# A plain weight tile between the two passes of an output projection, and raw weights of every third pair in two other tiles

## The chip, the cores and the metric

The kernel runs on one core of one Trainium2 chip. The metric is the device time of one execution in microseconds (us); the reported time is the median of several executions. A core has a matrix engine (PE, with its weight loads shown apart as PEld), a vector engine (DVE), a scalar engine (ACT), a general engine (POOL) and a queue engine (SP) that issues most DMAs here. Each engine works through its own instruction list in order and waits on semaphores.

## The reference

One encoder layer over 512 tokens of width 1024, in float32:

```python
h = swiglu(rmsnorm(x, g1), w1_in, w1_out);  x = x + 0.5 * rmsnorm(h, g1p)      # D_FF = 2816
h = mixer(rmsnorm(x, gm), ...);             x = x + rmsnorm(h, gmp)            # convolution and mLSTM heads
h = swiglu(rmsnorm(x, g2), w2_in, w2_out);  x = x + 0.5 * rmsnorm(h, g2p)
def swiglu(x, w_in, w_out):
    gate, up = split(x @ w_in, 2);  return (silu(gate) * up) @ w_out
```

The two feed-forward blocks (function `ffn`, called twice) hold the work that the change touches; the mixer lies between them and is not touched.

## The kernel before

**Products.** Each float32 operand is split into a rounded high part and a low remainder (`split`: a CAST on ACT for the high part, a subtraction on DVE, L327, for the low part), and a product is three matmuls: high by high, high by low, low by high. `split_free` (L331, L332) is the same with no fixed order. On top of this both projections of a block use a seven-product scheme (as in Strassen's method) for most of the weights, with the combinations of operands formed by DVE subtractions.

**Input projection.** The 2816 hidden columns are 22 tiles of 128 (`NF`); the first two (`PLAIN`) are multiplied plainly (L491), the other 20 (j = 2 to 21) with seven products of 12 matmuls of 256 columns each (`mm_part`, L468). For each j a pair of raw weight tiles (gate g and up u, 512 KB each) is loaded by SP (L178) into two tiles of the pool `rawp`, which has four; `w_pair` (L190, with `split`) makes the operands out of them on DVE and ACT, and the raw tiles are free again when its last split has read them. So the load of a pair waits for the pair two before it.

**Output projection.** The 22 hidden tiles are the contraction. `OUT` lists the order: eight items "a" (a0 to a7, the first pass), then "b" items (the second pass) and plain items "k". An a takes two rows of weights and does products 1, 6, 7, 5; a b takes the second of these rows again and does products 2, 3, 4 (`product_out`, L613; six matmuls of 512 columns to a product). A k multiplies one hidden tile plainly into all eight PSUM banks (`mm_out`, L637, 24 matmuls). With `SEVEN` = 8 and `TAIL` = 5 the order is a0 ... a7, b0, k16, b1 ... b7, k17 ... k21, and k17 to k21 are multiplied at the end, one block of 128 tokens after the other.

**Between the passes.** The eight PSUM banks hold sums of the first pass that must be read out and partly subtracted before the second pass overwrites or goes on with them. `taken(n)` does it after each product of a7: for product 1 a copy on ACT (L623), for 6, 7 and 5 two subtractions each on DVE (L572, `big<-ps,big`), six in all. Product 4 restarts the banks of product 7 and k16 those of product 6; products 2 and 3 go on in the banks of 1 and 5. `left_b` forms the left factors of a group of two b's: one split of 1024 elements (L332 on DVE), one subtraction (L572), one split of 512; `w_out_b` splits the weights of one b (1024 and 512 elements, L327).

**Who orders the instructions.** The program is written in one order; a planner with a timeline model of its own then orders each engine's list, taking an instruction early when its model says it is ready. `pin` ties an instruction behind the one that the program traced just before it on the same engine. `tc.issue_after(x)` ties what a block traces on x's engine behind x. Both set the order in the engine's list only. A new tile of a pool waits until an old one of the pool is free.

**The two idle tiles.** The pool `t4p` has two tiles (`t4()`). In a block they hold normalised inputs, then `v1` and `v3` in `combine_x` (L398), then nothing but `own2` (raw rows for a0 and a1, L159) and the scratch `s1` of `left_a`.

Of the kernel before, what the change touches and what calls it, by code (L numbers as in the profile page):

```python
# [8 lines left out]
F32 = mybir.dt.float32  # L9
# [7 lines left out]
P = 128  # L17
# [8 lines left out]
DV = 128  # L26
EPS = 1e-6
NEG = -1e30
TAIL = 5
SEVEN = 8  # L30
WARM = 20
WARM2 = 4
ON_POOL = (0, 1, 2, 3)
PLAIN = 2
BW = 528


@with_exitstack
def encoder_kernel(ctx: ExitStack, tc: tile.TileContext, a: dict, out: bass.AP):
# [15 lines left out]
    def nm(s):  # L55
        uid[0] += 1
        return f"{s}_{uid[0]}"
# [47 lines left out]
        return [v[0]], v[1]  # L105


    OUT = [("a", i) for i in range(SEVEN)]
    for i in range(SEVEN):
        OUT += [("b", i)] + [("k", 2 * SEVEN + i)] * (2 * SEVEN + i < NF - TAIL)  # L110
    OUT += [("k", k) for k in range(2 * SEVEN, NF) if ("k", k) not in OUT]

    stream = []
    for w_in, w_out in ((w1i, w1o), (w2i, w2o)):
        if w_in is w2i:
            stream += [(wm[blk(i, 2 * P), V0:V0 + 512].rearrange("(k p) f -> p k f", p=P), 2) for i in range(4)]
            stream += [cols(wm, c) for c in (Q0, Q0 + P, K0, K0 + P)]
            stream += [cols(wm, O0 + i * P) for i in range(4)]
            stream += [cols(wm, CG)]
            for i in range(4):  # L120
                stream += [cols(wm, c + i * P) for c in ((CG, HC, BG) if i else (HC, BG))]
            stream += [rows(wo, k * P) for k in MIXK[:5]]
        for j in range(NF):
            pair = [cols(w_in, j * P), cols(w_in, DFF + j * P)]
            stream += pair if j < PLAIN else [([v[0] for v in pair], KD)]
        for kind, n in OUT:
# [8 lines left out]
    pos, done = [0], [0]  # L135

    def w_load(n):
        for _ in range(n):
            if pos[0] < len(stream):
# [27 lines left out]
                if kk == "b":  # L167
                    nc.gpsimd.dma_start(kept[0], aps[0][:, 0:512], accum_op=ALU.add)
                    aps = [aps[0]]
                    own = [kept.pop(0)]  # L170
                else:
                    own = []
                for ap in aps:
                    raw = rawp.tile([P, 1024], F32, tag="raw", name=nm("raw"))
                    if isinstance(kk, str):
                        nc.sync.dma_start(raw[:, 1024 - ap.shape[1]:], ap)
                    else:
                        nc.sync.dma_start(raw if kk == 1 else raw.rearrange("p (k f) -> p k f", k=kk), ap)  # L178
                    raws.append(raw)
# [292 lines left out]
    def ffn(xq, between, finish, mid=None, within=None, ahead=(2, 2, 1, 1), late=None, prep=None):  # L472

# [97 lines left out]
        def tt(o, a_, b_, op, order=lambda v: None):  # L571
            order(nc.vector.tensor_tensor(out=o, in0=a_, in1=b_, op=op))  # L572
# [9 lines left out]
            return [{n: (hi[:, i, c:c + 256], lo[:, i, c:c + 256]) for n, c in at.items()} for i in range(g)]  # L582

        def group(i):
            g = min(2, SEVEN - i)
# [15 lines left out]
        def left_b(i):  # L601
# [4 lines left out]
            split_free(hi[:, :, 512:768], lo[:, :, 512:768], a_[:, :, early])  # L606
            return parts(hi, lo, g, {4: 0, 2: 256, 3: 512})

        def product_out(n, left, right, first, last_):
            tb, half = bank[n]  # L610
            for t in range(2):
                for x, y in ((0, 0), (0, 1), (1, 0)):
                    nc.tensor.matmul(  # L613
                        acc[tb + t][half], left[n][x][:, blk(t)], right[n][y], start=first and x == y == 0,
                        stop=last_ and x == 1, skip_group_check=True)

        def taken(n):

            for t in range(2):
                o = acc[bank[n][0] + t][bank[n][1]]  # L620
                e12, e22, e21 = extra[2 + t, 1], extra[t, 1], extra[t, 0]
                if n == 1:
                    nc.scalar.copy(e12, o)  # L623
                elif n == 5:
                    tt(e22, o, e21, ALU.subtract, pin)
                elif n == 6:
                    tt(e12, o, e12, ALU.subtract, pin)
                else:
                    tt(e21, o, e12, ALU.subtract, pin)

        begun = set()

        def mm_out(tb, half, k, hT, w):
            fresh = (tb, half) in ((0, 1), (1, 1)) and (tb, half) not in begun
            begun.add((tb, half))
            for hh, ww in ((0, 0), (0, 1), (1, 0)):
                nc.tensor.matmul(  # L637
                    acc[tb][half], hT[hh][:, blk(tb)], w[ww][:, blk(half, 512)],
                    start=fresh and hh == ww == 0, stop=k == NF - 1 and hh == 1, skip_group_check=True)
# [12 lines left out]
            acc[at[0]][at[1]] = ps()  # L652
        hs, plain_n = None, 0
        ks = {}
        for at, (kind, n) in enumerate(OUT):
            if kind == "k":
                if plain_n % 2 == 0:
                    hs = bigt(F32R)
                q = 2 * (plain_n % 2)
                plain_n += 1  # L660
                hT = (hs[:, q, 0:512], hs[:, q + 1, 0:512])
                split(hT[0], hT[1], hcol(n))
                ks[n] = (hT, w_get(min(2, len(OUT) - 1 - at)))
                if plain_n == 1 and mid:
                    mid()
                if n < NF - TAIL:
                    for tb in range(NT):
                        for half in range(2):
                            mm_out(tb, half, n, *ks[n])
            elif kind == "a":  # L670
                if n % 2 == 0 and n:
                    lefts = left_a(n)
                left, right = lefts[n % 2], w_get(1)
                for m in ((1, 6, 7, 5) if n else (6, 7, 5)):
                    product_out(m, left, right, n == 0, n == SEVEN - 1)
                    if n == SEVEN - 1:
                        taken(m)
            else:
                if n % 2 == 0:
                    lefts = left_b(n)  # L680
                left, right = lefts[n % 2], w_get(2)
                for m in (2, 3, 4):
                    product_out(m, left, right, n == 0 and m == 4, False)

        ring.clear()
        pinned["rest"] = False
# [11 lines left out]
        if prep:  # L698
            prep()
        for tb in range(NT):  # L700
            todo = [(half, k) for half in ((1, 0) if tb == NT - 1 else (0, 1)) for k in range(NF - TAIL, NF)]
# [505 lines left out]
    def store(tb, h):  # L1207
        nc.sync.dma_start(out[0, blk(tb), h], x_t[tb][:, h])

    ffn(xT3, {(3, 2): lambda: flip_q(3, xs[3], xT3)}, lambda tb, acc: post_norm(tb, acc, g_post3, 4.0, store, (1, 0) if tb == NT - 1 else (0, 1)))  # L1210


_INS = [
# [26 lines left out]
```

## Time and profile before

| what | value |
|---|---|
| runs of the kernel | 899.17, 899.81, 902.55 us; median 899.81 |
| the profiled execution, by its own time | 899.46 us |
| its span, first to last instruction | 897.1 us |
| first input projection, L468 | about 38 to 236 us |
| first output projection | about 234 to 351 us |
| second input projection, L468 | about 571 to 780 us |
| second output projection | about 780 to 891 us |

A row of the timeline is: start in us, time covered in us, engine, line and operation, tile written <- tiles read, shape, count; in square brackets the idle time of the engine before it and who ended it. Successive matmuls overlap: a matmul of 512 columns is shown with some 0.39 us, though the next one starts some 0.23 us after it. A wait for several semaphores is put down to the one that came last.

### The profile page before, as it was taken

To read this page: it belongs to the slowest core of one execution; us is meant where nothing else is said; L and a number is where in the kernel's file an instruction comes from. 1 tells how busy PE (TensorE), PEld (TensorE's weight loads), DVE (VectorE), ACT (ScalarE), POOL (GpSimd) and SP (SyncE) were. 2 spreads that over 40 slices of the span, in tenths; PEclk is the share of its full clock that TensorE was granted. 3 is DMA by queue.
4 is the path that set the end of the run, shared out by engine and by line. 5 is a ranking of instruction groups with operands and counts; after the bars stand their busy time and mean duration, and the time that the engine had idled before them with its cause. 6 is when DMAs were issued, how large, how long until landed. Compare 5 with 4: busy or idle time off the path is not lost.

```text
span 897.1 us, 14998 instructions
## 1 busy us (share of the span) xinstructions
PE 886.2 (99%) x5935; PEld 806.9 (90%) x5935; DVE 696.8 (78%) x1081; ACT 469.9 (52%) x803; POOL 77.7 (9%) x100
## 2 busy tenths in 40 slices
PE   9999999999999999999999999999999999999997
PEld 7999999999987888988888888999999999987885
DVE  5988988888898777574666736889788888898755
ACT  6645555555547644464555435654554555657521
POOL 5000000001140111100011000000000000222000
PEclk9999999999999999999999999999999999999999
DMA  8434443434798570433222601324334334899402
GB/s 237 115 95 119 120 116 105 130 98 123 194 214 224 164 211 1 123 90 94 71 72 71 191 20 50 112 71 123 95 104 126 101 94 136 195 230 228 151 25 93
DMA packets 136079, 110.61 MB, mean 123 GB/s; under 512 B 5045, under 2 KB 115657, under 8 KB 136010
## 3 DMA queue, kind: packets, MB, share of 16 engines
q1 hardware_dynamic: 129354, 97.09, 36.5%
q0 software_dynamic: 6656, 12.58, 8.2%
q8 instruction: 46, 0.75, 0.3%
q14 instruction: 23, 0.19, 0.1%
HBM read 107.56 MB, written 2.10 MB: 122 GB/s over the span
## 4 chain that ended last, share of the span: by engine, by line
PE 82%; DVE 8%; DMA 6%; ACT 2%; issue 2%; POOL 0%; DVEq 0%; POOLq 0%; SPq 0%; ACTq 0%
PE ps L468 40%; PE ps L459 12%; PE ps L613 7%; PE ps L637 7%; PE ps L1197 5%; PE ps L491 4%; DVE wlo L327 3%; PE ps L819 3%; DMA raw<-in_w_ffn_out_dram 2%; DMA t<-in_w_ffn_out_dram 2%; DMA raw<-in_w_ffn_in_dram 2%; DVE big L332 1%; DVE big L572 1%; ACT whi L324 1%; PE ps L1112 1%
## 5 line engine op out<-in xcount | busy, mean ns | idle before, releaser
L468 PE MATMUL ps<-big,whi 128*128 128x256 f32 x1920 | 265.0, 280 | 0.7 <-ACT whi L324 0.7
L324 ACT CAST whi<-raw 128x1024 fp32r<-128x1024 f32 x197 | 202.4, 1051 | 114.3 <-DVE raw L190 46.7
L327 DVE TENSOR_TENSOR wlo<-raw,whi 128x1024 fp32r<-128x1024 f32 x193 | 233.6, 1219 | 35.5 <-ACT whi L324 20.2
L468 PEld LDWEIGHTS ps<-big,whi 128*128 128x128 f32 x1920 | 243.0, 188 | 1.3 <-ACT whi L324 1.1
L468 PE MATMUL ps<-big,wlo 128*128 128x256 f32 x960 | 151.6, 280 | 0.0
L468 PEld LDWEIGHTS ps<-big,wlo 128*128 128x128 f32 x960 | 129.7, 188 | 0.0
L613 PE MATMUL ps<-whi,big 128*128 128x512 f32 x384 | 122.2, 390 | 0.5 <-DVE big L572 0.3
L613 PEld LDWEIGHTS ps<-whi,big 128*128 128x128 f32 x384 | 71.8, 188 | 16.2 <-DVE big L572 0.9
L459 PE MATMUL ps<-big,whi 128*128 128x512 f32 x320 | 78.3, 397 | 0.0
L613 PE MATMUL ps<-wlo,big 128*128 128x512 f32 x192 | 74.8, 389 | 0.0
L459 PEld LDWEIGHTS ps<-big,whi 128*128 128x128 f32 x320 | 59.5, 188 | 13.7 <-issue 0.2
L468 PE MATMUL ps<-big,ws 128*128 128x256 f32 x480 | 65.6, 280 | 0.0
L637 PE MATMUL ps<-whi,big 128*128 128x512 f32 x192 | 60.7, 394 | 0.4 <-DVE big L327 0.4
L468 PEld LDWEIGHTS ps<-big,ws 128*128 128x128 f32 x480 | 60.4, 188 | 0.0
L148 POOL DMA_DIRECT2D raw<-in_w_ffn_out_dram x16 | 19.6, 1222 | 442.6 <-DMA raw<-in_w_ffn_out_dram 212.7
L543 ACT COPY t<-ps 128x256 f32<-128x256 f32 x40 | 14.9, 372 | 68.6 <-PE ps L468 68.6
L637 PEld LDWEIGHTS ps<-whi,big 128*128 128x128 f32 x192 | 35.8, 188 | 8.9 <-DVE big L327 1.0
L613 PEld LDWEIGHTS ps<-wlo,big 128*128 128x128 f32 x192 | 36.0, 188 | 7.4
L459 PE MATMUL ps<-big,wlo 128*128 128x512 f32 x160 | 40.4, 395 | 0.0
L637 PE MATMUL ps<-wlo,big 128*128 128x512 f32 x96 | 37.1, 393 | 0.0
L331 ACT CAST big<-big 128x512 fp32r<-128x512 f32 (+1 forms) x32 | 26.0, 837 | 20.2 <-DVE big L332 10.4
L459 PEld LDWEIGHTS ps<-big,wlo 128*128 128x128 f32 x160 | 30.0, 188 | 7.0
(214 smaller groups left out, 1240.0 us busy)
## 6 DMA issues: line engine op xcount, KB each, us to landing
raw<-in_w_ffn_in_dram SPq DMA_DIRECT2D x88, 512.0 KB, 4.5
raw<-in_w_ffn_out_dram SPq DMA_DIRECT2D x28, 512.0 KB, 4.7
raw<-in_w_mix_in_dram SPq DMA_DIRECT2D x24, 512.0 KB, 5.5
raw<-in_w_ffn_out_dram SPq DMA_DIRECT2D x32, 256.0 KB, 5.5
raw<-in_w_ffn_out_dram POOLq DMA_DIRECT2D x16, 512.0 KB, 7.7
raw<-in_w_mix_out_dram SPq DMA_DIRECT2D x8, 512.0 KB, 3.5
big<-in_w_ffn_out_dram SPq DMA_DIRECT2D x12, 256.0 KB, 6.6
big<-in_w_ffn_out_dram POOLq DMA_DIRECT2D x8, 256.0 KB, 8.8
```

The source lines that it names most:

```text
L148: nc.gpsimd.dma_start(sums.rearrange("p (g f) -> p g f", g=2), top[:, 512:1024].rearrange("p (g f) -> p g f", g=1).broadcast_to([P, 2, 512 ...
L324: latest["hi"] = nc.scalar.copy(out=hi, in_=src)
L327: latest["lo"] = eng.tensor_tensor(out=lo, in0=src, in1=f32(hi), op=ALU.subtract)
L331: nc.scalar.copy(out=hi, in_=src)
L459: nc.tensor.matmul(o, ww[:, k, :], xk(xT, xx, k, sl), start=n == 0, stop=n == 3 * KD - 1)
L468: pin(nc.tensor.matmul(o, ww[:, k, :], x[xx][:, k, :], start=first and n == 0, stop=n == 11, skip_group_check=True))
L491: pin(nc.tensor.matmul(o, ww[:, k, :], xq_hl(xq, (k // 4, th))[xx][:, k % 4, :], start=n == 0, stop=n == 3 * KD - 1))
L543: nc.scalar.copy(a_[:, h1], x[:, h0])
L613: nc.tensor.matmul(acc[tb + t][half], left[n][x][:, blk(t)], right[n][y], start=first and x == y == 0, stop=last_ and x == 1, skip_group_c ...
L637: nc.tensor.matmul(acc[tb][half], hT[hh][:, blk(tb)], w[ww][:, blk(half, 512)], start=fresh and hh == ww == 0, stop=k == NF - 1 and hh == ...
L819: nc.tensor.matmul(pv_[i][:, 0:at.stop - at.start], xk(xT, xx, k, blk(tb)), ww[:, k % 2, at], start=n == 0, stop=n == 3 * KD - 1)
L1197: nc.tensor.matmul(acc[half], yy[yi][:, k % 4, blk(tb)], wmo[k][wi][:, blk(half, 512)], start=(n == 0 and yi == 0 and wi == 0), stop=(n == ...
```

## The change

Three edits, in both blocks. First, the order of the output projection is made by a function of its own, in which one plain item stands between the two passes: a0 ... a7, k16, b0 ... b7, k17 ... k21. k16 goes through the banks in another order: those of product 1, of 6, of 7, of 5. The `start` flags, which clear a bank, follow: k16 restarts the banks of 6 and 7, and product 4 restarts its banks only if no plain item has. Second, `left_b` is queued on DVE behind the last of the six subtractions (`mark["taken"]`). Third, the raw weights of pairs 3, 6, 9, 12 and 15 of each block's 20 are loaded into two `t4` tiles and not into `rawp`. `SPLIT` replaces `SEVEN` and `TAIL` with the same values for both blocks.

```diff
+    def out_order(seven, tail):
+        v = [("a", i) for i in range(seven)]
+        v += [("k", 2 * seven)] * (2 * seven < NF - tail)
+        for i in range(seven):
+            v += [("b", i)] + [("k", 2 * seven + i + 1)] * (2 * seven + i + 1 < NF - tail)
+        return v + [("k", k) for k in range(2 * seven, NF) if ("k", k) not in v]
...
+                third = False
+                if len(aps) == 2:
+                    pairs[0] += 1
+                    third = pairs[0] % (NF - PLAIN) in THIRD
                 for ap in aps:
-                    raw = rawp.tile([P, 1024], F32, tag="raw", name=nm("raw"))
+                    raw = t4() if third else rawp.tile([P, 1024], F32, tag="raw", name=nm("raw"))
...
+        begun = {(t, 0) for t in (2, 3)} | {(t, 1) for t in (2, 3)}
+
         def product_out(n, left, right, first, last_):
             tb, half = bank[n]
             for t in range(2):
+                if n == 4:
+                    first = (t, 0) not in begun
+                    begun.add((t, 0))
...
                 elif n == 5:
-                    tt(e22, o, e21, ALU.subtract, pin)
+                    tt(e22, o, e21, ALU.subtract, lambda v: (pin(v), mark.update(taken=v)))
...
-            fresh = (tb, half) in ((0, 1), (1, 1)) and (tb, half) not in begun
+            fresh = (tb, half) not in begun
...
-                    for tb in range(NT):
-                        for half in range(2):
-                            mm_out(tb, half, n, *ks[n])
+                    for tb, half in ((2, 0), (3, 0), (0, 1), (1, 1), (0, 0), (1, 0), (2, 1), (3, 1)):
+                        mm_out(tb, half, n, *ks[n])
...
-                    lefts = left_b(n)
+                    with tc.issue_after(mark["taken"].ins):
+                        lefts = left_b(n)
                 left, right = lefts[n % 2], w_get(2)
                 for m in (2, 3, 4):
-                    product_out(m, left, right, n == 0 and m == 4, False)
+                    product_out(m, left, right, False, False)
```

More of the change, by code (lines that the diff above doesn't have):

```diff
@@ L28 @@
 NEG = -1e30
-TAIL = 5
-SEVEN = 8
+SPLIT = ((8, 5), (8, 5))
 WARM = 20
@@ L35 @@
 BW = 528
+THIRD = (3, 6, 9, 12, 15)
 @with_exitstack
@@ L105, in one @@
         return [v[0]], v[1]
[L108 to L111, printed above, removed]
+    def out_order(seven, tail):
[4 more added lines that the diff above has]
+        return v + [("k", k) for k in range(2 * seven, NF) if ("k", k) not in v]
     stream = []
@@ L125, in encoder_kernel @@
             stream += pair if j < PLAIN else [([v[0] for v in pair], KD)]
-        for kind, n in OUT:
+        for kind, n in out_order(*SPLIT[w_in is w2i]):
             if kind == "a":
@@ L134, in encoder_kernel @@
     loaded, ready, ring, own2 = [], [], [], []
-    pos, done = [0], [0]
+    pos, done, pairs = [0], [0], [0]
     def w_load(n):
@@ L470, in mm_part, with ffn @@
                 n += 1
-    def ffn(xq, between, finish, mid=None, within=None, ahead=(2, 2, 1, 1), late=None, prep=None):
+    def ffn(xq, between, finish, mid=None, within=None, ahead=(2, 2, 1, 1), late=None, prep=None, block=0):
+        seven, tail = SPLIT[block]
+        order = out_order(seven, tail)
         h = [bigt() for _ in range((NF + 3) // 4)]
@@ L584, in group @@
         def group(i):
-            g = min(2, SEVEN - i)
+            g = min(2, seven - i)
             v = h[i // 2].rearrange("p (g e) f -> p g e f", e=2)[:, 0:g, :, 0:512]
@@ L629, in taken @@
                     tt(e21, o, e12, ALU.subtract, pin)
-        begun = set()
         def mm_out(tb, half, k, hT, w):
-            fresh = (tb, half) in ((0, 1), (1, 1)) and (tb, half) not in begun
+            fresh = (tb, half) not in begun
             begun.add((tb, half))
@@ L654, in ffn @@
         ks = {}
-        for at, (kind, n) in enumerate(OUT):
+        for at, (kind, n) in enumerate(order):
             if kind == "k":
@@ L662, in ffn @@
                 split(hT[0], hT[1], hcol(n))
-                ks[n] = (hT, w_get(min(2, len(OUT) - 1 - at)))
+                ks[n] = (hT, w_get(min(2, len(order) - 1 - at)))
                 if plain_n == 1 and mid:
                     mid()
-                if n < NF - TAIL:
-                    for tb in range(NT):
-                        for half in range(2):
-                            mm_out(tb, half, n, *ks[n])
+                if n < NF - tail:
+                    for tb, half in ((2, 0), (3, 0), (0, 1), (1, 1), (0, 0), (1, 0), (2, 1), (3, 1)):
+                        mm_out(tb, half, n, *ks[n])
             elif kind == "a":
@@ L674, in ffn @@
                 for m in ((1, 6, 7, 5) if n else (6, 7, 5)):
-                    product_out(m, left, right, n == 0, n == SEVEN - 1)
-                    if n == SEVEN - 1:
+                    product_out(m, left, right, n == 0, n == seven - 1)
+                    if n == seven - 1:
                         taken(m)
@@ L700, in ffn @@
         for tb in range(NT):
-            todo = [(half, k) for half in ((1, 0) if tb == NT - 1 else (0, 1)) for k in range(NF - TAIL, NF)]
+            todo = [(half, k) for half in ((1, 0) if tb == NT - 1 else (0, 1)) for k in range(NF - tail, NF)]
             if tb == NT - 1 and mid:
@@ L1208, in store @@
         nc.sync.dma_start(out[0, blk(tb), h], x_t[tb][:, h])
-    ffn(xT3, {(3, 2): lambda: flip_q(3, xs[3], xT3)}, lambda tb, acc: post_norm(tb, acc, g_post3, 4.0, store, (1, 0) if tb == NT - 1 else (0, 1)))
+    ffn(xT3, {(3, 2): lambda: flip_q(3, xs[3], xT3)}, lambda tb, acc: post_norm(tb, acc, g_post3, 4.0, store, (1, 0) if tb == NT - 1 else (0, 1)), block=1)
 _INS = [
```

## The prediction, written before the changed kernel was timed

> **What bounds the kernel now.** I read the profile page first, then the table of waits on PE, then the chain that ended last, and then the timeline of PE, DVE, ACT and SP around each wait.
>
> ```profile
> span 897.1 us, 14998 instructions
> PE 886.2 (99%) x5935; PEld 806.9 (90%) x5935; DVE 696.8 (78%) x1081; ACT 469.9 (52%) x803; POOL 77.7 (9%) x100
> PEclk9999999999999999999999999999999999999999
> ```
>
> ```profile
> PE ps L613 <- DVE big L572: 1.8, 3, 1.2
> ...
> PE ps L468 <- ACT whi L324: 0.7, 2, 0.5
> ...
> PE ps L637 <- DVE big L327: 0.4, 1, 0.4
> ```
>
> ```profile
> 583.70 187.90 PE ps L468 x1596
> ...
> 863.43 27.64 PE ps L637 x120
> ```
>
> The reader is to see that PE is the bound nearly from end to end, at a granted clock that never falls, and that its waits are few. In undisturbed stretches a 256-column matmul takes 187.90 / 1596 = 0.118 us of PE and a 512-column one 27.64 / 120 = 0.230 us. The change leaves the number and the shapes of the matmuls as they are, so it can only win what PE loses in waits, here and there. The three rows of waits on PE (columns: us in total, times, longest) are those that it aims at. They count idle time after the shown end of a matmul. As the next matmul could have started some 0.16 us before that end (0.39 shown less 0.23; 0.28 less 0.118 for the narrow ones), each wait costs 0.16 us more than its row.
>
> ```profile
> 827.34 0.39 PE L637 MATMUL ps<-whi,big 128*128 128x512 f32 x1
> 827.57 0.39 PE L637 MATMUL ps<-wlo,big 128*128 128x512 f32 x1
> 829.17 0.97 PE L613 MATMUL ps<-wt,big 128*128 128x512 f32 x3 [1.22 <-DVE big L572]
> ```
>
> In block 2 the step from 827.57 to 829.17 is 1.60 us where 0.23 (827.34 to 827.57) is usual: 1.37 lost. The rest of the first and last row of waits, 1.8 - 1.22 in two waits and 0.4 in one, is block 1's, by its timeline between 286 and 290 us: 0.58 + 0.4 + 3 x 0.16 = 1.46 lost. All four waits lie where the first pass of an output projection goes over into the second.
>
> ```profile
> 70.33 0.63 PE L468 MATMUL ps<-big,wlo 128*128 128x256 f32 x4
> 71.15 2.03 PE L468 MATMUL ps<-big,whi 128*128 128x256 f32 x15 [0.19 <-ACT whi L324]
> ...
> 81.58 0.62 PE L468 MATMUL ps<-big,whi 128*128 128x256 f32 x3 [0.46 <-ACT whi L324]
> ```
>
> ```profile
> 68.73 0.69 DVE L190 TENSOR_TENSOR t<-raw 128x512 f32<-128x512 f32 x1 [1.87 <-DMA raw<-in_w_ffn_in_dram]
> 69.33 0.68 DVE L190 TENSOR_TENSOR raw<-raw 128x512 f32<-128x512 f32 x1
> ```
>
> ```profile
> 70.05 2.00 ACT L324 CAST whi<-raw 128x1024 fp32r<-128x1024 f32 x2 [2.27 <-DVE raw L190]
> ```
>
> ```profile
> 62.95 5.75 DMA raw<-in_w_ffn_in_dram
> ```
>
> The other two waits are in the first input projection, and together cost 0.19 + 0.46 + 2 x 0.16 = 0.97 us. Read backwards: PE waits for a cast of pair 4 (70.05), this for a DVE subtraction of pair 4 (69.33), and this stands in DVE's list behind the first addition of pair 5 (68.73), which waits 1.87 us for pair 5's raw weights. Their load could start only at 62.95, when pair 3 gave back its `rawp` tiles, and took 5.75 us.
>
> **The change part by part.**
>
> *k16 between the passes.* It moves 24 matmuls of 0.23 us, 5.5 us of PE work, ahead of b0. What PE waits for today is this:
>
> ```profile
> 821.49 0.69 DVE L572 TENSOR_TENSOR big<-ps,big 128x512 f32<-128x512 f32 x1 [0.49 <-PE ps L613]
> 822.10 1.82 DVE L332 TENSOR_TENSOR big<-big,big 128x1024 fp32r<-128x1024 f32 x2
> 823.83 1.22 DVE L327 TENSOR_TENSOR wlo<-raw,whi 128x1024 fp32r<-128x1024 f32 x1
> 824.97 1.28 DVE L572 TENSOR_TENSOR big<-ps,big 128x512 f32<-128x512 f32 x2
> 826.16 1.22 DVE L327 TENSOR_TENSOR wlo<-raw,whi 128x1024 fp32r<-128x1024 f32 x1
> 827.30 1.22 DVE L332 TENSOR_TENSOR big<-big,big 128x1024 fp32r<-128x1024 f32 x1
> 828.43 0.68 DVE L572 TENSOR_TENSOR big<-ps,big 128x512 f32<-128x512 f32 x1
> 829.03 0.68 DVE L332 TENSOR_TENSOR big<-big,big 128x512 fp32r<-128x512 f32 x1
> ```
>
> The six subtractions (`big<-ps,big`) are spread over DVE's list with left factors of the second pass (L332) and weight splits (L327) between them; the fourth begins at 828.43 and PE goes on at 829.17. From start to start a 1024-element step costs DVE 1.13 us (827.30 to 828.43) and a 512-element one 0.60. Call T the end of a7 on PE: the first subtraction starts when 9 of a7's 24 matmuls are through, so T is some 15 x 0.23 = 3.4 us later, near 824.8. With the left factors tied behind them, the first four subtractions fit between 821.5 and T, and the sixth is over near T + 0.9. PE has k16 from T on: the high parts in the banks of product 1 need no subtraction, those of 6 and 7 are free by then, and those of 5 come last, 18 x 0.23 = 4.1 us after T. So all four waits go: 1.46 + 1.37 = 2.83 us. Price: nothing, as long as DVE has b0's operands by T + 5.5.
>
> *The low half of k16's left factor* is pinned behind the sixth subtraction: ready at T + 0.9 + 0.6 = T + 1.5. Two of three matmuls per bank do not need it, 16 x 0.23 = 3.7 us of cover. I cost it at nothing; uncovered it would be 1.5 us.
>
> *left_b behind the subtractions.* Behind the sixth stand k16's low half (0.60), b0's weights (1.13 + 0.60), b1's (1.13 + 0.60), and `left_b` for both (1.13 + 0.60 + 0.60): 6.4 us of DVE in all, done by T + 7.3. PE asks for product 2 at T + 5.5 and for product 3 at T + 6.9. If the planner puts the first split of `left_b` straight behind b0's weights it is there at T + 0.9 + 0.6 + 1.7 + 1.1 = T + 4.3, and the wait is nil. If b1's weights come first, it is T + 6.0: 0.5 us lost, and about as much again at product 3, whose factor needs a subtraction, a cast and a split more. Both ends: 0 and 1.0 us per block. I take 0, since the rows above show the planner putting L332 ahead of b1's split (826.16). Later b's ask DVE for about 1.7 + 1.2 us each against 18 x 0.23 = 4.1 of PE.
>
> *DMA.* Here the stretch is tight, but the loads of k16 and b0 only change places:
>
> ```profile
> 800.00:830.00 30.00, 28.78 (x128) 23.51 (x127) 25.91 (x34) 20.63 (x29) 5.97 (x6) 1.00 0.97 246
> ```
>
> ```profile
> 262.68 0.33 SPq L176 DMA_DIRECT2D raw<-in_w_ffn_out_dram  x1
> 267.00 0.33 SPq L178 DMA_DIRECT2D raw<-in_w_ffn_out_dram  x1
> ```
>
> (The first row's last two columns are DMA share and GB/s.) Both are one 512 KB load in the same `rawp` slot; k16's takes b0's place at 262.68, more than 20 us ahead of the waits near 286 us, and b0, whose half-row addition runs on POOL's queue, is wanted 5.5 us later than today. No cost. The small load that the first plain item triggers in block 1 moves one b earlier; no PE work of this stretch reads it.
>
> *Pairs 3, 6, 9, 12, 15 in t4.* While these are among the pairs, a load waits for the pair three before it, not two. Pair 5's load then waits for pair 2, not for the 62.95 release, and would be there before DVE asks at 68.73; the same goes for the wait at 81.58. Both ends: 0 and 0.97 us won; I take 0.97, for pair 5's load gains about a whole pair, 84 x 0.118 = 9.9 us, against a lateness of 1.87. Since a third pair's predecessor in `rawp` is never asked for later than now, no load can be much later than today, with one exception, pair 3 itself:
>
> ```profile
> 40.39 1.22 DVE L327 TENSOR_TENSOR big<-t,big 128x1024 fp32r<-128x1024 f32 x1
> ...
> 46.50 0.68 DVE L190 TENSOR_TENSOR t<-raw 128x512 f32<-128x512 f32 x1
> ...
> 49.78 1.22 DVE L327 TENSOR_TENSOR wlo<-raw,whi 128x1024 fp32r<-128x1024 f32 x1
> ```
>
> ```profile
> 52.00 0.63 PE L468 MATMUL ps<-big,wlo 128*128 128x256 f32 x4
> ```
>
> Its second tile is free only after the last read of `v3` (40.39 + 1.2 = 41.6); with 5.75 us of load it lands near 47.4, when DVE asks at 46.50. That pushes the split at 49.78 by up to 0.9 us; it would end at 51.9, and PE reads it at 52.00. Cost 0, or up to 0.9 if that margin is missing.
>
> The Trainium skill, "Perfetto Trace Analysis" (section Optimization Strategy), says that a gap that repeats on the engine that should be saturated can mean too few buffers. This trace agrees for two pairs of block 1 alone; by that rule a gap of 0.49 us in each of 40 pairs would be worth 19 us, and the trace, with 1596 matmuls of block 2 at an even 0.118, excludes that.
>
> **Sum.** 1.46 + 1.37 + 0.97 = 3.8 us, against the profiled execution's 899.46 (897.1 span and 2.4 around it): 895.7. That execution lies 0.35 below the median of the runs, 899.81; from the median it is **896.0**, 0.42% less. A measurement of this kernel tells about 0.5%, 4.5 us, from no change.
>
> **The rivals.**
>
> *1. b0's factors become the wait.* For it: DVE is busy 25.9 of 30 us in that stretch, and one strict list holds 6.4 us of work behind the sixth subtraction against 5.5 us of cover. Against: the planner's order today. Price 1.0 us per block: 896.0 + 2.0 = 898.0. The Trainium skill, "PSUM — Partial Sum Buffer" (section Engine vs sequencer instructions), says that VectorE's queue is strictly first in, first out; the rows above, an addition that waits for DMA with a subtraction of another pair behind it, agree, and by that rule this rival decides.
>
> *2. The extra tiles do nothing* (the planner, seeing loads earlier, moves the next pair's addition forward as well, and DVE waits as before): 896.0 + 0.97 = 897.0.
>
> *3. Slower: the first pass becomes DVE's.* `left_a`'s scratch is a t4 tile; today one is free early in the projection, in spare DVE time, and the third pairs now hold it until pair 15 is split. If the planner then puts this work (two steps of 0.60 us) and the splits of a0's and a1's rows (two of 0.60) into the full stretch,
>
> ```profile
> 245.00:255.00 10.00, 10.00 (x46) 8.28 (x45) 10.00 (x15) 4.87 (x8) 4.27 (x4) 1.00 0.81 181
> ```
>
> where DVE shows 10.00 of 10 us, PE follows: 2.4 us per block, 4.8 in all, 896.0 + 4.8 = 900.8. It decides only if nothing of this is done between the split of pair 15 and a0; that are five pairs, 5 x 9.9 us, and DVE is busy 78% of the span, so about 11 us of it are free there. That speaks against it. To go over 904.3 takes 8.3 us of new waits, for which I find no row.
>
> *4. Faster than the bound*: everything above and another 0.7 us. No wait row quoted here holds that much more; what speaks for it is that the runs themselves lie 0.64 us apart at the low end (899.17 and 899.81), and that the planner may close a small wait of the first pass on the way: 895.0.
>
> **How the numbers follow.** Forecast 0.52 (895.3 to 897), rival 1 0.16, rival 2 0.09, rival 3 0.05, a new plan somewhere that costs over 8 us 0.05, rival 4 0.13. Faster by over 0.5% (under 895.3) is rival 4: 0.13. Slower by over 0.5% is the new plan: 0.05. Within: 0.82. The range keeps the forecast, rivals 1 and 2, the ends of the unknown costs (0.9 for pair 3, 2.0 for b0) and half of rival 4: 894.8 to 900.0.
>
> **What would show it.** Between the passes PE's wait on L572 and L327 gone in both blocks, 24 L637 matmuls in a row before the first of b0, the six subtractions next to each other on DVE; PE's wait on L324 at pairs 4 and 5 gone, DVE's waits for raw weights between 57 and 80 us gone. Wrong if PE waits for L332 or a b's weights some 5.5 us after a7, if DVE still waits for raw weights there, or if the output projection's first pass shows new PE waits.

## The result and the profile after

| | before | after |
|---|---|---|
| median of the runs | 899.81 us (11 runs, 897.52 to 902.55) | 895.31 us (11 runs, 892.51 to 897.48) |
| ratio, 95% interval | | 0.9943 (0.9927 to 0.9959) |
| the profiled execution, by its own time | 899.46 us | 896.0 us |
| its span | 897.1 us | 894.0 us |

One run of all those below, the sixth of e6 (967.69 us at a mean granted clock of 0.85, where the others show 0.99 to 1.00), is left out of every ratio.

The change makes the kernel 0.57% faster (0.41 to 0.73). A second measurement of the same code, below as e4_after_again, gave 0.48% (0.34 to 0.61). The median lies in the predicted range and 0.7 us under the predicted 896.0. "Within 0.5%" had been given most of the chance, and the two measurements lie on both sides of that line. The intervals are some 0.16% wide to each side, so a difference well under the 0.5% that the prediction took as the least one to be told can be told here.

The head of the profile page of after, and of the chain that ended last the shares by engine (before, this row began with PE 82%, DVE 8%, DMA 6%, ACT 2%):

```profile
span 894.0 us, 15004 instructions
...
PE 886.2 (99%) x5935; PEld 806.9 (90%) x5935; DVE 696.9 (78%) x1081; ACT 471.7 (53%) x803; POOL 81.8 (9%) x100
...
PEclk9999999999999999999999999999999999999999
...
PE 98%; issue 1%; ACT 0%; DVE 0%; DVEq 0%; POOLq 0%; POOL 0%; ACTq 0%
```

PE does the same 5935 matmuls in the same busy time. What changed is its waits. The table of waits on PE, whole (its one row stands in the table of before as well, there with L317):

```profile
PE ps L323 <- POOL rawg L315: 1.3, 1, 1.3
```

None of the three rows that the prediction started from is left, in either block. (After has its own line numbers: L468 is now L474, L613 is L627, L637 is L649, L572 is L581, L332 is L338, L327 is L333, L190 is L196, L178 is L184. The copies on ACT, L623, are now L637, which in before is the line of the k items' matmuls.) Between the passes of block 2 the timelines of DVE and of PE now read:

```profile
819.36 0.68 DVE L581 TENSOR_TENSOR big<-ps,big 128x512 f32<-128x512 f32 x1
821.33 3.08 DVE L581 TENSOR_TENSOR big<-ps,big 128x512 f32<-128x512 f32 x5 [1.29 <-ACT big L637]
824.32 0.68 DVE L333 TENSOR_TENSOR big<-big,big 128x512 fp32r<-128x512 f32 x1
824.92 1.22 DVE L333 TENSOR_TENSOR wlo<-raw,whi 128x1024 fp32r<-128x1024 f32 x1
826.06 1.22 DVE L338 TENSOR_TENSOR big<-big,big 128x1024 fp32r<-128x1024 f32 x1
```

```profile
821.12 0.39 PE L649 MATMUL ps<-whi,big 128*128 128x512 f32 x1
...
823.61 0.40 PE L649 MATMUL ps<-wlo,big 128*128 128x512 f32 x1
823.87 0.50 PE L649 MATMUL ps<-whi,big 128*128 128x512 f32 x1
824.20 0.40 PE L649 MATMUL ps<-wlo,big 128*128 128x512 f32 x1
824.46 0.50 PE L649 MATMUL ps<-whi,big 128*128 128x512 f32 x1
824.80 0.40 PE L649 MATMUL ps<-wlo,big 128*128 128x512 f32 x1
825.06 2.13 PE L649 MATMUL ps<-whi,big 128*128 128x512 f32 x8
827.03 0.62 PE L627 MATMUL ps<-whi,big 128*128 128x512 f32 x2
```

The reader is to see three things. The six subtractions stand together, with no left factor or weight split among them. PE works on k16 from 821.12 to 827.03 while DVE does them. And k16 is not quite even: from 823.61 on the steps are 0.26, 0.33, 0.26, 0.34, 0.26 us where 0.227 is usual. These three long steps lose some 0.4 us, and the table of waits doesn't show them. PE follows the subtractions closely there; that these are the cause is read from the times alone.

In the first input projection, SP's loads of pair 3 (second tile) and pair 5, and DVE's work around the first addition of pair 5:

```profile
41.66 0.37 SPq L184 DMA_DIRECT2D t<-in_w_ffn_in_dram  x1
51.00 2.19 SPq L184 DMA_DIRECT2D raw<-in_w_ffn_in_dram  x2
```

```profile
65.75 0.68 DVE L196 TENSOR_TENSOR t<-raw 128x512 f32<-128x512 f32 x1
```

Pair 5's second load lay at 62.95 before and now goes out by 53.2 (51.00 + 2.19); its first addition no longer waits for DMA.

**Stages.** To compare kernels without their rows of waits, this table gives distances between the starts of two PE matmuls, worked out from the traces. "Pairs" goes from the first to the 841st matmul of the seven-product part of block 1's input projection; "a4 to a7" from the 97th to the 192nd of the first pass; "transition" from the last matmul of a7 to the last of b7 (by count, the 192nd and the 336th product matmul), k16 included. Nowhere waiting, the last one takes 168 steps of 0.2271 us, 38.15 us, and the shortest seen are 38.16.

| us | before | after |
|---|---|---|
| pairs, block 1 | 100.05 | 98.82 |
| a4 to a7, block 1 / 2 | 21.99 / 21.53 | 21.97 / 22.08 |
| transition, block 1 / 2 | 40.32 / 39.78 | 38.77 / 39.02 |

So before lost 2.16 and 1.62 us in the transitions, and after still loses 0.61 and 0.86. The three stages that the change aims at give 1.23 + 1.55 + 0.76 = 3.5 us. With the row of a4 to a7, where after takes 0.5 longer, the table gives 3.0, and the two spans differ by 3.1. The two profiled executions differ by 3.46 in their own times: 0.3 us of that lies outside the spans, where this table can't see it.

### The profile page after: what moved, and what is told of

It reads as the page before. It is cut to its first block, busy times and chain, and to the rows that moved or that the text cites. A ratio compares the mean times of both kernels' runs of the same rounds, so it can differ in the third digit from the quotient of the medians.

```text
span 894.0 us, 15004 instructions
## 1 busy us (share of the span) xinstructions
PE 886.2 (99%) x5935; PEld 806.9 (90%) x5935; DVE 696.9 (78%) x1081; ACT 471.7 (53%) x803; POOL 81.8 (9%) x100
## 4 chain that ended last, share of the span: by engine, by line
PE 98%; issue 1%; ACT 0%; DVE 0%; DVEq 0%; POOLq 0%; POOL 0%; ACTq 0%
PE ps L474 44%; PE ps L627 16%; PE ps L465 13%; PE ps L649 7%; PE ps L500 5%; PE ps L1209 5%; PE ps L831 3%; PE ps L386 1%; PE ps L1124 1%; PE ps L323 1%; PE ps L326 0%; PE ps L434 0%; PE ps L1132 0%; PE ps L1073 0%; PE ps L1100 0%
## 5 line engine op out<-in xcount | busy, mean ns | idle before, releaser
L474 PE MATMUL ps<-big,whi 128*128 128x256 f32 x1920 | 264.2, 280 | 0.0
L474 PEld LDWEIGHTS ps<-big,whi 128*128 128x128 f32 x1920 | 242.7, 188 | 0.2
L330 ACT CAST whi<-raw 128x1024 fp32r<-128x1024 f32 x167 | 172.0, 1051 | 96.1 <-DVE raw L196 28.8
L333 DVE TENSOR_TENSOR wlo<-raw,whi 128x1024 fp32r<-128x1024 f32 x163 | 197.5, 1219 | 22.7 <-PE ps L465 8.7
L474 PE MATMUL ps<-big,wlo 128*128 128x256 f32 x960 | 151.2, 280 | 0.0
L474 PEld LDWEIGHTS ps<-big,wlo 128*128 128x128 f32 x960 | 129.5, 188 | 0.0
L627 PE MATMUL ps<-whi,big 128*128 128x512 f32 x384 | 120.5, 390 | 0.2
L627 PEld LDWEIGHTS ps<-whi,big 128*128 128x128 f32 x384 | 71.9, 188 | 15.8 <-ACT whi L330 1.1
L627 PE MATMUL ps<-wlo,big 128*128 128x512 f32 x192 | 74.3, 390 | 0.0
L474 PE MATMUL ps<-big,ws 128*128 128x256 f32 x480 | 65.2, 280 | 0.0
L649 PE MATMUL ps<-whi,big 128*128 128x512 f32 x192 | 61.2, 396 | 0.0
L474 PEld LDWEIGHTS ps<-big,ws 128*128 128x128 f32 x480 | 60.2, 188 | 0.0
L333 DVE TENSOR_TENSOR wlo<-t,whi 128x1024 fp32r<-128x1024 f32 (+1 forms) x42 | 44.7, 1067 | 5.3 <-ACT whi L330 4.9
L330 ACT CAST whi<-t 128x1024 fp32r<-128x1024 f32 (+1 forms) x42 | 38.0, 926 | 17.0 <-DVE t L196 9.7
L649 PEld LDWEIGHTS ps<-whi,big 128*128 128x128 f32 x192 | 35.8, 188 | 9.3 <-DVE big L581 0.8
L627 PEld LDWEIGHTS ps<-wlo,big 128*128 128x128 f32 x192 | 36.0, 188 | 7.8 <-DVE wlo L333 0.3
L649 PE MATMUL ps<-wlo,big 128*128 128x512 f32 x96 | 37.7, 393 | 0.0
```

The lines of the kernel that those rows point to most:

```text
L330: latest["hi"] = nc.scalar.copy(out=hi, in_=src)
L333: latest["lo"] = eng.tensor_tensor(out=lo, in0=src, in1=f32(hi), op=ALU.subtract)
L474: pin(nc.tensor.matmul(o, ww[:, k, :], x[xx][:, k, :], start=first and n == 0, stop=n == 11, skip_group_check=True))
L627: nc.tensor.matmul(acc[tb + t][half], left[n][x][:, blk(t)], right[n][y], start=first and x == y == 0, stop=last_ and x == 1, skip_group_c ...
L649: nc.tensor.matmul(acc[tb][half], hT[hh][:, blk(tb)], w[ww][:, blk(half, 512)], start=fresh and hh == ww == 0, stop=k == NF - 1 and hh == ...
```

## The experiments

Three theories were held against each other, the third of them only from e9 on. A: the gain is the sum of the PE waits removed, some 3.8 us, and nothing else. B: in other executions the kernel before waits longer for raw weights than in the profiled one, so that the loads are worth more. C: the end of the first pass waits for DMA by an amount that differs from one execution to the next, whatever the kernel. Ratios are against runs of the kernel before on the same chip, with 95% intervals; their medians were 899.89, 899.67 and 899.9 us in the three groups of four.

### The kernel before, profiled again

No edit.

> The kernel before, once more, against itself. Theory A (the win is the sum of the PE waits that the profiles show to be gone; what lies beyond that sum is the spread of executions): ratio 1.000 within 0.002, a profiled span of 895 to 900 us, and the same PE waits as in the first profile: between the passes about 1.5 us in block 1 and 1.4 in block 2, and about 1.0 us for pairs 4 and 5. Theory B (the kernel before waits longer for raw weights in other executions than in the profiled one, so the change wins more than that sum): the waits for pairs 4 and 5 or in the first pass differ by over 1 us from the first profile.

Measured: median 900.22 us of 12, ratio 1.001 (0.9999 to 1.0021). The profiled execution was the slowest of its runs, 902.99 us, 3.5 us more than the one shown first. Pairs take 99.81 us here, transitions 40.35 and 39.79: as before. The difference lies in a4 to a7 of block 2, 25.61 instead of 21.53. From the table of waits on PE, and PE's timeline there:

```profile
PE ps L613 <- ACT whi L324: 2.5, 2, 2.2
```

```profile
812.42 0.39 PE L613 MATMUL ps<-whi,big 128*128 128x512 f32 x1
815.00 1.30 PE L613 MATMUL ps<-whi,big 128*128 128x512 f32 x4 [2.19 <-ACT whi L324]
816.10 0.63 PE L613 MATMUL ps<-wlo,big 128*128 128x512 f32 x1
816.52 0.63 PE L613 MATMUL ps<-whi,big 128*128 128x512 f32 x1
816.95 0.63 PE L613 MATMUL ps<-wlo,big 128*128 128x512 f32 x1
817.38 2.23 PE L613 MATMUL ps<-whi,big 128*128 128x512 f32 x5
819.45 0.39 PE L613 MATMUL ps<-wlo,big 128*128 128x512 f32 x1
```

The wait on ACT's cast is one for weights. A load on POOL's queue that adds part of an a's weights to a tile already loaded (L148, 512 KB) takes 10.3 us from issue to landing here and 7.4 in the first profile. Until it lands DVE and ACT stand; the cast that PE waits for follows at 813.90. The issue and DVE's next step, here and then in before:

```profile
803.50 1.20 POOL L148 DMA_DIRECT2D raw<-in_w_ffn_out_dram  x1 [5.73 <-DMA raw<-in_w_ffn_out_dram]
813.86 0.69 DVE L232 TENSOR_TENSOR t<-big,raw 128x512 f32<-128x512 f32 x1 [4.67 <-DMA raw<-in_w_ffn_out_dram]
```

```profile
804.08 1.20 POOL L148 DMA_DIRECT2D raw<-in_w_ffn_out_dram  x1 [5.91 <-DMA raw<-in_w_ffn_out_dram]
811.54 0.69 DVE L232 TENSOR_TENSOR t<-big,raw 128x512 f32<-128x512 f32 x1 [1.94 <-DMA raw<-in_w_ffn_out_dram]
```

What follows: by the sign written down beforehand, a first pass that differs by over 1 us counts for B, and A had expected the same waits and a span of at most 900 us, where 900.8 was measured. The waits of the pairs, which the tiles aim at, are no larger here (99.81 against 100.05), and the seven traces without these tiles all have 99.6 to 100.5. So B holds for a stage that the change doesn't touch and not for the one that would make the loads worth more. This is where C comes from: one wait of 2.2 us is there in one execution and not in another. How 2.2 us of it become 4.08 is told in the last section.

### The extra tiles alone

```diff
+THIRD = (3, 6, 9, 12, 15)
-                    raw = rawp.tile([P, 1024], F32, tag="raw", name=nm("raw"))
+                    raw = t4() if third else rawp.tile([P, 1024], F32, tag="raw", name=nm("raw"))
```

> The kernel before with only the t4 tiles for pairs 3, 6, 9, 12, 15. Theory A: PE's waits on the casts of pairs 4 and 5 go and nothing else changes: 1.0 to 1.3 us less, ratio 0.9985, the waits between the passes as before. Theory B: 2.5 us less or more, ratio at most 0.997.

Measured: 899.77 us of 12, ratio 0.9998 (0.9986 to 1.0011): nothing. Pairs take 98.82, so their 1.23 us are won. The transition of block 2 takes 40.59, 0.81 longer than before, and that of block 1 takes 39.78, 0.54 shorter. From a4 to a7 the two blocks take 22.15 each, 0.8 longer together. PE's waits:

```profile
PE ps L618 <- DVE big L577: 1.8, 3, 1.2
...
PE ps L618 <- ACT whi L329: 0.6, 2, 0.3
...
PE ps L642 <- DVE wlo L332: 0.2, 1, 0.2
```

The wait on the subtractions (L577 is before's L572) is unchanged, and new small ones stand beside it. The planner has made another order of the transitions, although no line of them was edited; the longest wait now lies in block 1. What follows: the pairs are worth at least what their rows say. The new plan takes back 0.27 of it in the transitions, and the end of the first pass 0.8 in this execution, where it differs between executions anyway (e1). By the stages 0.2 us are left, by the medians nothing.

### The order of the output projection alone

The changed kernel with `THIRD = ()`.

> The changed kernel with all raw weights in rawp (no t4 tiles). Theory A: the waits between the passes go, those of pairs 4 and 5 stay: 2.0 to 3.0 us less than before, ratio 0.997. Theory B: at most 2 us less, ratio 0.998 or more, the rest of the win being the t4 tiles'.

Measured: 896.89 us of 8, ratio 0.9963 (0.9951 to 0.9975). Transitions 39.01 and 38.56, that is 1.31 + 1.22 = 2.5 us won; pairs 100.45, not won. What follows: the order is the larger part of the change. With the tiles on top the ratio is 0.9943 or 0.9952, with intervals that overlap this one; the tiles add 1.0 us by the ratios and 1.6 by the medians of e3 and e4, and the pairs' stage shows 1.63.

### The changed kernel again

No edit.

> The changed kernel once more. Theory A: ratio 0.994 to 0.996, equal to the product of the two part ratios within 0.0015; profiled span 890 to 895. Theory B: the same total, but with e2's share the larger one.

Measured: 895.31 us of 5, ratio 0.9952 (0.9939 to 0.9966). Pairs 98.81, transitions 38.45 and 38.72. By stages the change gives 1.24 + 1.87 + 1.06 = 4.2 us here and 3.5 in the first profile.

### k16 between the passes, without the tie

e3 without the order on DVE:

```diff
-                    with tc.issue_after(mark["taken"].ins):
-                        lefts = left_b(n)
+                    lefts = left_b(n)
```

> k16 between the passes with its new bank order, but left_b not tied behind the subtractions, and no t4 tiles (e3 without the tie). Theory A (the tie is what lets the subtractions go first): left factors (L338) stand between the six subtractions again, PE waits on L581 come back in part, and the stretch from the end of a7 to the last b is over 39.3 us in at least one block (38.6 and 39.0 in the changed kernel, 40.3 and 39.8 before): ratio 0.998. Rival (5.5 us of k16 are cover enough whatever the order on DVE): that stretch as in e3, 39.0 and 38.6, ratio 0.9963.

Measured: 901.24 us of 12, ratio 1.002 (1.001 to 1.003). Transitions 40.68 and 40.43, longer than before the change. The wait has only moved from the b's to k16, as the table of waits on PE and DVE's timeline show:

```profile
PE ps L649 <- DVE big L581: 2.9, 4, 1.0
```

```profile
282.10 1.22 DVE L338 TENSOR_TENSOR big<-big,big 128x1024 fp32r<-128x1024 f32 x1
283.24 0.68 DVE L581 TENSOR_TENSOR big<-ps,big 128x512 f32<-128x512 f32 x1
283.84 0.68 DVE L338 TENSOR_TENSOR big<-big,big 128x512 fp32r<-128x512 f32 x1
```

Left factors (L338) still stand among the subtractions, and k16 needs those banks sooner than the b's did.

### The tie, without k16 between the passes

The kernel before with the order on DVE:

```diff
-                    tt(e22, o, e21, ALU.subtract, pin)
+                    tt(e22, o, e21, ALU.subtract, lambda v: (pin(v), mark.update(taken=v)))
-                    lefts = left_b(n)
+                    with tc.issue_after(mark["taken"].ins):
+                        lefts = left_b(n)
```

> The kernel before (b0, k16, b1 ..., no t4 tiles) with left_b tied behind the last subtraction. Theory A: without k16 ahead of it, b0 finds its left factor only some 2 us after a7 and its other one 1.5 us later; PE loses what it lost before or up to 2 us more in each block: ratio 1.000 to 1.005. Rival (the planner itself moves k16 ahead once left_b is late, so the tie alone is enough): ratio 0.997, the stretch from a7 to the last b under 39.3 us in both blocks.

Measured: ratio 1.0042 (1.0029 to 1.0056); five runs from 901.78 to 904.06 us. Transitions 42.54 and 42.42, 2.2 and 2.6 longer than before. The waits on PE:

```profile
PE ps L613 <- DVE big L332: 4.5, 4, 1.1
PE ps L637 <- DVE big L327: 1.6, 2, 0.8
```

Now the subtractions are early and the left factors (L332) late, with no work on PE meanwhile. What follows from e5 and e6 together: each half alone is a loss, and only both are a gain. This is the mechanism that the prediction described, with its first rival, factors that come too late, showing up where the cover is missing.

### k16 through the banks in the old order

e3 with the order of the banks that a k had before:

```diff
-                    for tb, half in ((2, 0), (3, 0), (0, 1), (1, 1), (0, 0), (1, 0), (2, 1), (3, 1)):
+                    for tb, half in ((0, 0), (0, 1), (1, 0), (1, 1), (2, 0), (2, 1), (3, 0), (3, 1)):
```

> e3 with k16 going through the banks in the old order of the program (by token block, then half). Theory A: the planner takes the matmuls whose banks are free first, in whatever order they are written: within 0.3 us of e3 in the stretch after a7, ratio 0.9963. Rival (the order of the banks is part of the win): 1 us or more lost per block, ratio 0.998 or more.

Measured: 895.61 us of 7, ratio 0.9956 (0.994 to 0.9973), not apart from e3. But both transitions take exactly 38.16: nothing is lost in them. DVE and PE in block 2:

```profile
820.65 0.69 DVE L581 TENSOR_TENSOR big<-ps,big 128x512 f32<-128x512 f32 x1 [0.78 <-PE ps L627]
821.76 3.08 DVE L581 TENSOR_TENSOR big<-ps,big 128x512 f32<-128x512 f32 x5 [0.41 <-ACT big L637]
```

```profile
822.65 0.39 PE L649 MATMUL ps<-whi,big 128*128 128x512 f32 x1
...
826.27 2.03 PE L649 MATMUL ps<-whi,big 128*128 128x512 f32 x8
828.14 0.62 PE L627 MATMUL ps<-whi,big 128*128 128x512 f32 x2
```

Here the last subtraction ends 2.2 us after k16 starts (821.76 + 3.08 - 822.65); in after it is 3.3 (821.33 + 3.08 - 821.12). What follows: the new order of the banks is not needed for the gain. All eight transitions with the new order (after, e3, e4, e8) lose something, 0.13 to 0.86 us; of the eight with the old one (e7, e9, e10, e11) six lose nothing, one 0.18 and one 0.87. Each edit brings another plan, so the order of the banks and the plan are not told apart.

### Extra tiles in block 1 only

```diff
-                    third = pairs[0] % (NF - PLAIN) in THIRD
+                    third = pairs[0] in THIRD
```

> The changed kernel with the t4 tiles in block 1 only. Theory A: the waits of pairs 4 and 5 exist in block 1 alone, so nothing is lost: first input projection as in the changed kernel (98.8 us from pair 1 to pair 11), the stretch after a7 in block 2 back from 39.0 to e3's 38.6; ratio 0.994 to 0.995. Rival (the t4 tiles win something in block 2 that the profile does not show as a wait): slower than the changed kernel, ratio 0.996 or more.

Measured: 894.07 us of 6, ratio 0.9942 (0.9927 to 0.9958). Pairs 98.82, transitions 38.90 and 38.29. What follows: block 2 doesn't need the tiles: its pairs take 110.14 us here and in before, 110.15 with the tiles. Block 2 takes 0.7 less in its transition than the first profile of after.

### Both of these together

e8 with the old order of the banks.

> The parts that won, together: k16 between the passes, left_b tied, the old order of the banks, t4 tiles in block 1 only. Theory A (the parts add up): pairs 1 to 11 in 98.8 us as in the changed kernel, the stretch after a7 38.2 us in both blocks as in e7, no PE wait on DVE between the passes: ratio 0.9935, a median 0.5 to 1 us below the changed kernel's. Rival (the last tenths are noise): within 0.3 us of the changed kernel.

Measured: 894.62 us of 6, ratio 0.9932 (0.9911 to 0.9953). Pairs 98.82, transitions 38.34 and 38.16: by these stages 1.23 + 1.98 + 1.62 = 4.8 us better than before, the most of all versions that compute the whole result. The profiled execution gave 3.5 back in a4 to a7, which took 23.10 and 23.46 where 21.53 is the least. That is a wait for weights again, with DVE idle for 4.34 us until a DMA landed at 809.92:

```profile
PE ps L627 <- ACT whi L330: 2.9, 2, 1.6
```

### Two extra pairs instead of five

e9 with `THIRD = (3, 6)`.

> e9 with t4 tiles for pairs 3 and 6 of block 1 only. Theory A (only pairs 4 and 5 find their weights late, at the start of the projection): pairs 1 to 11 in 98.8 us, ratio as e9. Rival (the lead of three pairs has to be kept up): waits come back after pair 8, 0.5 us or more.

Measured: 894.72 us of 6, ratio 0.9943 (0.9925 to 0.9961). Pairs 98.81, transitions 39.03 and 38.16. What follows: in the pairs, 3 and 6 do all that the tiles do. e8, e9, e10 and the changed kernel can't be told apart by their medians.

### No half-row additions, with the best order and in the kernel before

In e9 and in the kernel before, the 256 KB loads that add to a tile already loaded (POOL's queue) are left out, and with them the lower half of the b's weights in the sums:

```diff
-                    nc.gpsimd.dma_start(kept[0], aps[0][:, 0:512], accum_op=ALU.add)
+                    pass
```

> e9 without the eight half-row additions per block that POOL's queue loads for the b items (256 KB read and added each): the lower half of these weights is left out of the sums. Theory C (the end of the first pass waits for DMA, by an amount that differs from execution to execution, and this is most of the spread of times): a4 to a7 takes 21.5 us in both blocks, the spread of the times is clearly under e9's, median 0.5 to 2 us lower. Rival (the spread comes from elsewhere, the start above all): same spread, same median within 0.3 us.

> The kernel before without these half-row additions (the same part left out). Theory C: a4 to a7 takes 21.5 us in both blocks (21.5 to 25.6 in the profiles of before so far), the median lies 0.5 to 2 us below before's, the waits between the passes stay at 40 us after a7 in each block. Rival: times and spread as before, ratio 1.000.

Measured: e11 893.33 us of 5 (891.54 to 893.57), ratio 0.9918 (0.99 to 0.9936). e12 897.68 of 10 (896.33 to 898.51), ratio 0.9974 (0.9962 to 0.9985). In both kernels a4 to a7 takes 21.53 in both blocks. In e12 the transitions are as before, 40.14 and 39.78, with the same row `PE ps L613 <- DVE big L572` of 1.8 us. The stretch around block 2's transition, of which the prediction showed before with a DMA share of 0.97, reads in e12:

```profile
800.00:830.00 30.00, 28.78 (x127) 23.26 (x126) 25.92 (x34) 19.82 (x27) 1.22 (x1) 1.00 0.64 167
```

What follows: C is borne out. Without these loads none of four readings of a4 to a7 is over 21.53; in the twelve traces with them, the two blocks together lie 0.1 to 4.7 us above twice that, 1.35 in the mean, and two profiles of the same kernel differ by 4.2. For before the loads cost about 2.2 us of median (899.9 - 897.68), 1.6 of it within the spans; for e9 it would be 1.3, but the intervals of e9 and e11 overlap. The spread of times says less: e12's runs lie within 2.2 us, those of before within 3.1 to 5.0 in four groups with more runs in each, and e3's, with the loads, within 2.2 too. Whether it is their bytes or their turn on POOL's queue that makes PE wait wasn't tried apart. The loads that PE waited for, those of the a's, stay in; in e12's trace the last three of them land no faster, 8.3 us in the median against 7.4, but the middle one is issued at 795.9 and not at 804.1, which speaks for the turn.

Between e11 and e12 lie 4.35 us of median, where the stages give 1.08 + 1.98 + 1.62 = 4.7: with the DMA wait out of the way, the time and what the stages win agree, as A says.

## Why the prediction was right or wrong

**The mechanism: right. The sum: close, in part by luck.** The prediction had 0.97 us from the pairs and 1.46 + 1.37 from the two transitions, 3.8 in all. The stages give 3.5 and 4.2 in two profiles of the changed kernel, and its median is 895.31, where 896.0 was written. The terms were less exact than their sum:

- *Pairs*, 0.97 predicted, 1.23 measured.
- *The two transitions*, 1.46 + 1.37 = 2.83 to be won; what before really lost there was 2.16 + 1.62 = 3.78. The four waits cost what the prediction said, 1.49 and 1.38 by the steps around them. What it put at nothing are steps that are longer without a row, up to 0.11 us each, before and behind the waits: 0.7 us in block 1 and 0.2 in block 2. In the timeline of before the three matmuls at 829.17, quoted in the prediction, are followed by

```profile
829.97 0.40 PE L637 MATMUL ps<-whi,big 128*128 128x512 f32 x1
```

  which is 0.80 us for three, where 0.68 is usual.
- *What the change leaves*: nothing was predicted, 0.61 + 0.86 was measured in the first profile, 0.29 + 0.56 in the second. One step that failed is the time of the sixth subtraction, "over near T + 0.9": it was over at T + 3.3. Only one of the six fitted before T, not four. The first was to start with 15 of a7's matmuls still to come; in e7, where it waits for PE, it starts 2.0 us before k16 (820.65 and 822.65), with nine to come. And the second waits for a copy on ACT, which the prediction didn't count (`[1.29 <-ACT big L637]` in after, 0.41 in e7). So k16's low half was ready at 824.32 + 0.68 = 825.0, T + 3.9, where T + 1.5 had been written. Its cover of 3.7 us was just about used up. The price was small, since the planner put k16's eight last matmuls behind it, from 825.06. In block 2 of after, 0.42 of the 0.86 lie in k16's long steps. The rest lies in the b's from 830.0 on, most of it in three steps of 0.34 us, and what these wait for stays open.

That the errors cancel is luck: 1.2 us more was there to be won (5.0 and not 3.8), and 0.85 to 1.5 of it was left.

**"Faster by over 0.5%": too small a chance.** The prediction gave this 0.13, since "no wait row quoted here holds that much more". The measured 0.57% and 0.48% lie at that line, so a chance near a half would have been fitting. The step that failed is to read what can be won from the rows of waits of a single execution, at 0.16 us beyond each row: 3.8 us predicted, where the traces of before had 1.23 + 3.78 = 5.0 to give, and e9 takes 4.8 of it.

A second term of the sum was held fixed without a reason: the "2.4 around it", between the span and the device time. In the 60 runs of before beside the experiments the device time is 2.1 to 2.5 us longer than the span, in the 16 runs of the changed kernel 1.8 to 2.0. That is 0.4 us of the 4.5 between the medians. Why it is so stays open; e6 has 2.0 and e12 1.7, so it isn't k16's place alone. What is left lies in the spans: beside e4 their medians are 897.55 and 893.4, 4.15 us apart, and the stages give 3.5 and 4.2. So the medians need nothing beyond these, and no B.

**k16 and the tie belong together: right.** e5 and e6 show each alone to be a loss (1.002 and 1.0042), both a gain (0.9963).

**The planner's order behind the sixth subtraction: right.** Low half, one weight split, then the first split of `left_b` at 826.06 is what the prediction took, and b0 had no wait that a row shows, although that split ended at T + 6.2 (826.06 + 1.22) and not at T + 4.3. Rival 1 decides only in e6, where k16 does not cover the factors; whether the long steps of the b's in after are a small part of it stays open.

**The new order of the banks** was costed as a help, its last banks coming late enough for the last subtractions. e7 loses nothing without it, so it isn't needed.

**The extra tiles: right in the pairs, incomplete beyond.** Pair 5's load went out about 10 us earlier, as written, and pair 3's exception cost nothing. Not foreseen was that a change of buffers in one stage makes the planner reorder another: in e2 the transition of block 2 pays 0.81, and that of block 1 wins 0.54. Rival 2, that the tiles do nothing, is what the median of e2 shows, but not for the reason given: the waits of the pairs went. Rival 3, a first pass bound by DVE, fell: from the last matmul of the input projection to the first of a4, PE takes 18.06 us for 80 matmuls in block 1 of before and 19.19 for 85 in block 1 of after, 0.226 each. Of the traces with the tiles only block 1 of e10 is longer there, by 0.65.

**The DMA of the output projection: no cost of the swap shows, but the stretch is not steady.** It was read from one execution with a DMA share of 0.97. In others PE waits there, 25.61 us instead of 21.53 in e1, and in e9 23.10 and 23.46: in the kernel before as in a version of the change.

## What to carry to other kernels

Work put between two dependent passes only helps if the engine that must free the buffers is told to do so first, and telling it so only helps if there is such work: try the two together, since each alone can lose. Where a planner orders the lists, compare every stage after an edit by the distance between fixed matmuls, not only the stage that was edited, for a better stage can be paid for in another and a row of waits doesn't show steps that are merely longer. For a gain of half a per cent, take two profiles of the kernel before you bound what there is to win: what differs between them is not yours to win or lose.

## What the runs showed of the hardware

**A wait of 2.2 us cost 4.1.** In e1 PE stood from 812.42 to 815.00, 2.35 more than a step. Behind it twelve matmuls took 4.45 us (815.00 to 819.45) where 2.72 is usual, steps of 0.42 among them. The granted clock in stretches of 5 us:

```profile
810.00:815.00 5.00, 2.81 (x13) 2.00 (x11) 1.14 (x2) 1.09 (x2) 2.81 (x3) 1.00 0.89 182
815.00:820.00 5.00, 5.00 (x15) 3.98 (x16) 3.97 (x7) 3.47 (x5) 0.88 (x1) 0.66 0.93 144
820.00:825.00 5.00, 5.00 (x24) 4.14 (x23) 2.78 (x3) 3.11 (x6) 0.87 (x1) 1.00 0.88 234
```

Third from the right: 1.00, 0.66, 1.00. So 2.35 + 1.73 = 4.08 us, which is the whole of 25.61 - 21.53. In e9 a wait of 1.63 us was followed by steps that were 0.12 longer in all, and the clock stayed:

```profile
811.06 1.19 PE L627 MATMUL ps<-whi,big 128*128 128x512 f32 x4 [1.63 <-ACT whi L330]
812.09 0.40 PE L627 MATMUL ps<-wlo,big 128*128 128x512 f32 x1
```

The Trainium skill, "TensorE: Matmul & The Clock Gate" (section HAM oscillation — how this bites in real kernels), gives idle gaps of more than about 3.4 us as what brings the clock down. The effect agrees, about half speed for a few us (steps of 0.42 against 0.227); the gap does not: here one of 2.19 us by its row was enough, and one of 1.63 was not. Nor does the length of one gap decide alone: from 5 to 10 us the mean clock is 0.75 in e2 and 0.79 in e12, with steps of 0.21 us where 0.11 had been reached, and the longest idle time in PE's rows nearby is 0.61 and 0.46 us.

**The start differs by 2 us.** The first matmul of the seven-product part starts between these two times in the fourteen traces, first that of e6, the earliest, then that of e3, the latest:

```profile
36.29 1.11 PE L468 MATMUL ps<-big,whi 128*128 128x256 f32 x8
```

```profile
38.52 1.10 PE L474 MATMUL ps<-big,whi 128*128 128x256 f32 x8
```

The difference is there from PE's first matmuls on. The same eight of 256 columns take, in e6 and in e3:

```profile
6.17 1.05 PE L317 MATMUL ps<-rawg 128*128 128x256 bf16 x8
```

```profile
7.72 1.89 PE L323 MATMUL ps<-rawg 128*128 128x256 bf16 x8
```

The six traces that start at 36.3 to 36.8 (e2, e6, e9 to e12) have steps of 0.11 us here, and the eight that start at 38.0 to 38.5 have 0.21, about half the speed. (This is read from the steps; the clock rows of e3 show 1.00 there.) Both profiles of before (38.37 and 37.98) and both of after (38.34) belong to the late ones. No kernel was profiled with both starts, so it isn't shown that the edits have no part in it; but e11's five runs lie at 891.5 and 891.7 and then at 893.3 to 893.6, two groups of one kernel that are as far apart. It is 0.2% of the time, in a stage that none of these kernels changes.
